# One activation table set in the front of a hybrid RWKV-7 and FoX trunk layer, with group norm, inverse and output split rearranged

## The chip, the cores and the metric

The kernel runs on one NeuronCore of one Trainium2 chip. The core has a matmul engine (PE; its weight loads are shown apart as PEld), a vector engine (DVE), an activation engine (ACT), GpSimd (POOL) and a queue that issues DMAs (SP). Each engine takes its own instructions in the order in which they were placed, and waits on semaphores for the others. The metric is device microseconds of one execution, the median of several runs; lower is better.

## The reference

One layer of a streaming encoder: 512 tokens after 16 meta tokens (T = 528), model width 1024, all in float32. After an RMS norm, one input projection of 5384 columns feeds two branches and the gates.

```
u = rmsnorm(h);  proj = u @ w_in
w_log = -softplus(-(w0 + tanh(wd) @ w_lora_up)) - 0.5        # decay of RWKV-7
decay = exp(-exp(w_log));  a = sigmoid(a0 + ad @ a_lora_up);  g = sigmoid(gd) @ g_lora_up
kk = k*k_k / max(||k*k_k||, 1e-12);  k = k*(1 + (a-1)*k_a)
S_t = S_{t-1}(diag(w_t) + a_t^T b_t) + v_t^T k_t;  y_t = S_t r_t     # 8 heads of 64
y_rw = (groupnorm(y)*lnx_g + lnx_b + bonus) * g
y_fx = softmax(q k^T/8 + F_q - F_k, causal) @ v              # FoX, 8 heads of 64, q and k normed
merged = sigmoid(gA)*(y_rw @ w_out_rw) + sigmoid(gB)*(y_fx @ w_out_fx)
h = h + merged @ w_o;  h = h + relu(rmsnorm(h) @ w_up)^2 @ w_down   # 4096 wide
```

## The kernel before

**Precision.** A float32 product of the large matmuls is made from three passes: each operand is split into a rounded part (hi, a cast on ACT) and the rest (lo, a subtraction on DVE or POOL), and PE adds hi*hi, hi*lo and lo*hi. `load_h` (L255) loads a weight tile of 128x512, casts it on ACT (L261) and subtracts on DVE (L262); `convert` (L466) does so for the input projection with the subtraction on POOL (L471, L472); `split` (L284) does it for activations (L285, L286).

**The front** (up to about 500 us) is a set of Python generators, "streams", that emit instructions in turns. `Turns.run` asks each stream, in order of rank, when the operands of its next piece will be ready; a planner (`Clock`) estimates that from a cost for each instruction emitted so far, without table loads. The first stream whose time plus `ROOM[rank]` has come goes on; a rank in `AHEAD` also has its DVE, ACT, POOL and DMA work placed earlier by that many steps of priority. PE's order is the order of emission and is never changed; the other engines are ordered by priority. The streams and their ranks:

- rank 0, `chain(g, prs)` (L939): the recurrence of a group of two head pairs over nine chunks of 64 tokens. A step fetches what was saved of the chunk from DRAM (`rec`, L948), multiplies with the state (L972), with the chunk's inverse (L978, `recs[pr_][hs, 448:]`), makes the new state (L990, L992) and the outputs (L998, L1001, L1002). For the second group it starts only when the first group's norm is finished (`yield normalised[0][1]`).
- rank 1, `recurrent` (L1040): for pairs 0 to 3 `decay` (two sigmoids, by `AF.Tanh` at L744, and the running product of decays), `keys`, `rows`, `scores`, and after every second pair `group`: `inverse(g, ...)` (L856), which inverts nine triangular matrices for each head into the tile `Tt` and saves them to `rec_d` in DRAM (`save(..., 448, 512, Tt)`), then adds the chain.
- rank 2, `attention`; rank 3, `fox_features` (norms of q and k, L570 to L575); rank 4, `group_norm` (L1008), called after chunks 4 and 8 of each chain; rank 8, `projections` (L476), 40 blocks of the input projection (matmuls at L500), of which the 16 gate blocks come last and fill what the others leave.
- rank 6, `fox_merged`: after the last projection it takes over the buffers `uhi` and `ulo` of the projection's input, splits `y_fx` into them (`part`), and multiplies with the FoX half of the output weights (L1103), gates the result (tanh at L1096, L1104) and writes it to DRAM (L1105). Rank 5, `rw_split`, splits `y_rw` into the same buffers as the group norms of group 1 finish.

**ACT's tables.** A function of ACT needs its table set loaded; a load is an instruction of its own on ACT (ACT_TABLE_LOAD). Before each Ln the kernel places a load of the set that has exp and ln (`pinned`, L280), after the instruction named, and the compiler adds further loads where an instruction's function isn't in the set that its order leaves there.

**After the front** the pools of the front are closed; then come the RWKV half of the output weights (L1151, with the gates' tiles `gl`), `w_o` (L1181, L1198) and the MLP (L1232, L1265).

Of the kernel before, what the change touches and what calls it, by code (L numbers as in the profile page):

```python
# [185 lines left out]
class Turns:  # L186
# [4 lines left out]
    AHEAD = {0: 100, 1: 40, 2: 20, 3: 20}  # L191
    ROOM = {0: 0.0, 1: 1.0, 2: 1.0, 3: 1.5, 4: 2.5, 5: 0.0, 6: 0.0, 8: 0.5}
# [32 lines left out]
def kernel(ctx, tc, ht, x, win, par, cst, gain, lora, wout, wo, wup, wdn, out, dbg=None):  # L225
# [24 lines left out]
    prh = cp.tile([128, 4, 4], F32, name="prh")  # L250
# [43 lines left out]
    rec_d = [dr.tile([NCH, 128, 512], F32, name=f"rec{i}") for i in range(4)]  # L294
# [5 lines left out]
    with ExitStack() as st:  # L300
# [103 lines left out]
        V.tensor_scalar(prh[:, 0, :], pr[:, C_W0:C_W0 + 4], 0.5, None, ALU.mult)  # L404
        V.tensor_scalar(prh[:, 1, :], pr[:, C_A0:C_A0 + 4], 0.5, None, ALU.mult)
        V.tensor_scalar(prh[:, 2, :], pr[:, C_KA:C_KA + 4], 0.5, None, ALU.mult)
        V.tensor_scalar(prh[:, 3, :], pr[:, C_KA:C_KA + 4], -0.5, 1.0, ALU.mult, ALU.add)
# [19 lines left out]
        act(gf, gf, AF.Tanh, scale=0.5)  # L427
# [108 lines left out]
        def fox_features():  # L536
            for p in range(4):
# [5 lines left out]
                def ask_normed(blk, parts, name):  # L543
                    d = {}

                    def begin():
# [4 lines left out]
                        def finish():  # L551
                            G.tensor_tensor(f, f, rs[:, c0:], ALU.mult)
                            d["s"] = act(sq[:, c0:], f, AF.Square)
# [8 lines left out]
                def normed(d, parts, gcol):  # L562
# [3 lines left out]
                    pin = None  # L566
                    for a0, a1 in parts:
                        pq = psm("pssq")[:, :a1 - a0]
                        for hs in hss:
                            mm(pq[hs], ones_blk[hs, hs], sq[hs, a0:a1], start=True, stop=True)  # L570
                        pin = pin or pinned(d["s"])
                        after(act(sq[:, a0:a1], pq, AF.Ln, bias=eps, scale=1.0 / 64), pin)
# [134 lines left out]
        normalised = [[Event(), Event()] for g in range(2)]  # L707

        class Pair:
# [20 lines left out]
            def decay(self):  # L730
# [6 lines left out]
                for a0, a1 in ((0, HT), (HT, T)):  # L737
# [5 lines left out]
                    for i in range(2):  # L743
                        act(dst[i][:, a0:a1], pos[i], AF.Tanh, bias=prh[:, i, p:p + 1], scale=0.5)  # L744
                V.tensor_scalar(dst[0], dst[0], 0.5, 0.5, ALU.mult, ALU.add)
# [8 lines left out]
            def keys(self):  # L754
# [4 lines left out]
                s_ = act(sq[:, :T], okr, AF.Square, scale=self.col(C_KK))  # L759
# [6 lines left out]
                pin = pinned(s_)  # L766
                after(act(sq[:, :T], sq[:, :T], AF.Ln), pin)
                act(sq[:, :T], sq[:, :T], AF.Exp, scale=-0.5)
                V.tensor_scalar(kp[:, PADT:], thr, prh[:, 2, p:p + 1], prh[:, 3, p:p + 1], ALU.mult, ALU.add)
# [5 lines left out]
                V.scalar_tensor_tensor(BK[:, :, 2, :], kkn, 0.5, pinv, ALU.mult, ALU.mult)  # L775
                V.scalar_tensor_tensor(BK[:, :, 0, :], tha3, 1.0, BK[:, :, 2, :], ALU.add, ALU.mult)
# [79 lines left out]
        def inverse(g, prs):  # L856
# [11 lines left out]
            if g > 0:  # L868
                for r0, r1 in low:
                    G.memset(Tt[r0, :, :, 32:64], 0.0)  # L870
# [23 lines left out]
            Tt2 = Tt.rearrange("p a b c -> p (a b) c")  # L894
            Dn, W2 = (AX_[:, i, :].rearrange("p (a b) -> p a b", b=64) for i in (1, 0))
# [33 lines left out]
            for pr_ in range(2):  # L929
# [7 lines left out]
                prs[pr_].save(slice(0, 128), 448, 512, Tt[:, pr_])  # L937

        def chain(g, prs):  # L939
# [4 lines left out]
            def fetch_rec(c):  # L944
                recs = []
                for q in prs:
                    t = rp.tile([128, 512], F32, name="rec", bufs=4)
# [16 lines left out]
            for c in range(NCH):  # L964
# [11 lines left out]
                for pr_ in range(2):  # L976
                    for hs in hss:
                        mm(ch[hs, 1, pr_, :], recs[pr_][hs, 448:], Rs[hs, pr_], start=True, stop=True)  # L978
# [24 lines left out]
                if c in (4, 8):  # L1003
                    turns.add(4, group_norm(g, y[:, :, c - 4:c, :], c - 4, prs, lws))
                if nxt is not None:
                    uv, recs = nxt, nxt_recs

        def group_norm(g, y, c0, prs, lws):  # L1008
# [9 lines left out]
            after(act(st2, st2, AF.Ln, bias=epsg, scale=1.0 / 64), pinned(s_))  # L1018
# [21 lines left out]
        def recurrent():  # L1040
# [4 lines left out]
            def group(g, ev):  # L1045
                yield from inverse(g, pairs[2 * g:2 * g + 2])
                turns.add(0, chain(g, pairs[2 * g:2 * g + 2]))
                ev.done = True
            pairs[0].ask_keys()
            pairs[0].ask_values()  # L1050
            for p, q in enumerate(pairs):
# [19 lines left out]
                if j == 1:  # L1071
                    turned_in = Event()
                    turns.add(1, group(g, turned_in))
            yield normalised[1][1]

        merge = []
        fox_split = Event()

        def part(k, c0, c1):
            split(merge[0][:, k, c0:c1], merge[1][:, k, c0:c1], (y_rw, y_fx)[k // 4][:, k % 4, c0:c1])  # L1080

        def fox_merged():

            yield projected
            for name in ("uhi", "ulo"):
                merge.append(up.tile([128, KB, S], F32R, name="y" + name, tag=name))
            turns.add(5, rw_split())
            for p in range(4):
                yield fox_done[p]
                part(4 + p, 0, S)  # L1090
            w = load_h(wout[0][:, 512:], V, "w", (WR, WH, WH))
            for m in range(KB):
                cur, w = w, load_h(wout[m + 1][:, 512:], V, "w", (WR, WH, WH)) if m < KB - 1 else None
                g = fp.tile([128, S], F32, name="gf", tag="qa", bufs=2)
                nc.sync.dma_start(g, gates_d[8 + m])
                act(g, g, AF.Tanh, bias=bgh[:, 8 + m:9 + m], scale=0.5)  # L1096
                po = None
                for k in range(4):
                    yield lambda f=po is None: max(ck.ready(*cur, merge[0][:, 4 + k, :], merge[1][:, 4 + k, :]), ck.ring("pj", 1, 2) if f else 0.0)
                    if po is None:  # L1100
                        po = ppj("pj")
                    for n, (a, b) in enumerate(passes([x[:, 128 * k:128 * k + 128] for x in cur], merge)):
                        mm(po, a, b[:, 4 + k, :], start=k == 0 and n == 0, stop=k == 3 and n == 2)  # L1103
# [3 lines left out]
        def rw_split():  # L1107
            for k in range(2):
                part(k, 0, S)
            for i in range(2):  # L1110
# [237 lines left out]
```

## Time and profile before

| | us |
|---|---|
| median of 3 runs (lowest to highest) | 932.55 (931.81 to 932.99) |
| the profiled execution, its own time | 933.79 |
| its span, first to last instruction | 932.0 |
| PE busy / DVE busy / ACT busy / POOL busy | 876.4 / 451.2 / 461.6 / 200.1 |
| mean granted clock of PE | 0.97 |

In the profile a group row reads: line, engine, operation, out<-in, shapes, count, then busy time, mean ns of one, idle time of the engine before them and what ended it. A wait row reads: who waited <- for whom: total us, times, longest. A row of stretches reads: stretch, its length, busy time of PE, PEld, DVE, ACT and POOL (with instructions), the granted PE clock, the DMA share and GB/s. A row of the timeline reads: start, duration, engine, line, operation. PE's busy time counts matmuls that overlap, so that a busy PE isn't a PE at its peak.

### The profile page before, as it was taken

The numbers are of one execution on the slowest core, as the hardware profiler recorded it, in microseconds if no ns is written. First come the engines' busy times: TensorE is split into PE (matmuls) and PEld (weight loads), VectorE is DVE, ScalarE is ACT, GpSimd is POOL, SyncE is SP. The second block draws the span as 40 slices with busy tenths as digits, with TensorE's granted clock in tenths as the row PEclk, the third lists the DMA queues.
The fourth block names the chain that finished last, engine by engine and source line by source line (L and its number), as shares of the span: only waits on it lengthen the run. The fifth ranks groups of instructions, "written<-read, shape, count | busy, mean of one in ns | idle before, by whom it ended". The sixth has DMA issues, their size and how long they took to land.

```text
span 932.0 us, 15719 instructions
## 1 busy us (share of the span) xinstructions
PE 876.4 (94%) x5968; PEld 717.4 (77%) x5968; DVE 451.2 (48%) x850; ACT 461.6 (50%) x941; POOL 200.1 (21%) x202
## 2 busy tenths in 40 slices
PE   7899898799898999999888899999999999999998
PEld 6888686587677877866566688988888888888886
DVE  6573546823546583345365665445423244543321
ACT  7755853765577536568554463344322234442220
POOL 1374453362515537231100210000000000000000
PEclk9999989899999999999989899999999999999999
DMA  6344246123574545234377760123223232322331
GB/s 218 93 124 129 63 115 169 39 95 103 162 213 137 119 133 179 66 112 135 115 236 260 249 215 12 46 95 98 99 94 102 91 102 94 99 101 92 119 97 46
DMA packets 94044, 113.26 MB, mean 122 GB/s; under 512 B 26888, under 2 KB 47624, under 8 KB 93968
## 3 DMA queue, kind: packets, MB, share of 16 engines
q1 hardware_dynamic: 93968, 112.25, 38.9%
q8 instruction: 47, 0.77, 0.3%
q14 instruction: 29, 0.24, 0.1%
HBM read 90.97 MB, written 20.07 MB: 119 GB/s over the span
## 4 chain that ended last, share of the span: by engine, by line
PE 68%; DVE 9%; ACT 9%; DMA 4%; issue 3%; POOL 3%; SPq 2%; POOLq 0%; ACTq 0%; DVEq 0%
PE po L1232 19%; PE pd L1265 19%; PE pj L500 11%; PE po L1181 3%; PE po L1198 2%; PE pj L1103 2%; DMA wraw<-in_win 2%; PE pw L907 1%; POOL wlo L472 1%; DVE tmp L889 1%; PE po L1151 1%; DVE AX L890 1%; ACT whi L471 1%; PE psc L637 1%; PE pj L390 1%
## 5 line engine op out<-in xcount | busy, mean ns | idle before, releaser
L261 ACT CAST whi<-wraw 128x512 fp32r<-128x512 f32 x152 | 93.8, 622 | 196.8 <-PE pd L1265 105.5
L262 DVE TENSOR_TENSOR wlo<-wraw,whi 128x512 fp32r<-128x512 f32 x152 | 104.3, 691 | 173.8 <-ACT whi L261 171.0
L500 PE MATMUL pj<-uhi,whi 128*128 128x264 f32 (+1 forms) x480 | 168.5, 351 | 3.2 <-ACT tm L328 3.2
L500 PE MATMUL pj<-uhi,wlo 128*128 128x264 f32 (+1 forms) x480 | 157.0, 327 | 0.0
L500 PE MATMUL pj<-ulo,whi 128*128 128x264 f32 (+1 forms) x480 | 157.0, 327 | 0.0
L472 POOL TENSOR_TENSOR wlo<-wraw,whi 128x512 fp32r<-128x512 f32 x80 | 107.7, 1358 | 127.1 <-ACT whi L471 109.4
L500 PEld LDWEIGHTS pj<-uhi,whi 128*128 128x128 f32 x480 | 93.1, 194 | 27.2 <-issue 13.2
L1265 PE MATMUL pd<-whi,fhi 128*128 128x512 f32 x256 | 99.6, 389 | 0.0
L1265 PE MATMUL pd<-wlo,fhi 128*128 128x512 f32 x256 | 99.6, 389 | 0.0
L1265 PE MATMUL pd<-whi,flo 128*128 128x512 f32 x256 | 99.6, 389 | 0.0
L500 PEld LDWEIGHTS pj<-uhi,wlo 128*128 128x128 f32 x480 | 93.0, 194 | 7.2
L500 PEld LDWEIGHTS pj<-ulo,whi 128*128 128x128 f32 x480 | 93.3, 194 | 5.0
L1232 PE MATMUL po<-zhi,whi 128*128 128x512 f32 (+1 forms) x248 | 94.8, 382 | 0.0
L1232 PE MATMUL po<-zlo,whi 128*128 128x512 f32 (+1 forms) x248 | 94.8, 382 | 0.0
L1232 PE MATMUL po<-zhi,wlo 128*128 128x512 f32 (+1 forms) x248 | 94.8, 382 | 0.0
L471 ACT CAST whi<-wraw 128x512 fp32r<-128x512 f32 x80 | 48.2, 620 | 33.2 <-DMA wraw<-in_win 18.2
L1265 PEld LDWEIGHTS pd<-wlo,fhi 128*128 128x128 f32 x256 | 48.0, 188 | 10.1
L1265 PEld LDWEIGHTS pd<-whi,flo 128*128 128x128 f32 x256 | 48.0, 188 | 9.9
L1265 PEld LDWEIGHTS pd<-whi,fhi 128*128 128x128 f32 x256 | 48.0, 188 | 9.9
L1232 PEld LDWEIGHTS po<-zhi,wlo 128*128 128x128 f32 x248 | 46.6, 188 | 9.1
L1232 PEld LDWEIGHTS po<-zlo,whi 128*128 128x128 f32 x248 | 46.6, 188 | 9.0
L1232 PEld LDWEIGHTS po<-zhi,whi 128*128 128x128 f32 x248 | 46.6, 188 | 8.9
(313 smaller groups left out, 1472.0 us busy)
## 6 DMA issues: line engine op xcount, KB each, us to landing
wraw<-in_win SPq DMA_DIRECT2D x84, 256.0 KB, 3.2
wraw<-in_wup SPq DMA_DIRECT2D x64, 256.0 KB, 2.6
wraw<-in_wdn SPq DMA_DIRECT2D x64, 256.0 KB, 2.5
rec<-rec SPq DMA_DIRECT2D x36, 256.0 KB, 3.0
gd<-gt SPq DMA_DIRECT2D x16, 256.0 KB, 2.1
wraw<-in_wout SPq DMA_DIRECT2D x16, 256.0 KB, 3.1
gl<-gd SPq DMA_DIRECT2D x16, 256.0 KB, 3.1
wraw<-in_wo SPq DMA_DIRECT2D x16, 256.0 KB, 4.8
```

The lines of the kernel that those rows point to most:

```text
L261: A.copy(hi, raw)
L262: low.tensor_tensor(lo, raw, hi.bitcast(F32), ALU.subtract)
L390: mm(dst, a, b[:, k, cols], start=n == 0, stop=n == 23)
L471: A.copy(hi, raw)
L472: G.tensor_tensor(lo, raw, hi.bitcast(F32), ALU.subtract)
L500: mm(po, a, b[:, k, a0:a1], start=n == 0, stop=n == 23)
L637: mm(sc, q[hs, 128 * i:128 * i + 128], k[hs, a:b], start=True, stop=True)
L1103: mm(po, a, b[:, 4 + k, :], start=k == 0 and n == 0, stop=k == 3 and n == 2)
L1181: mm(pd[i], a[:, k, 128 * i:128 * i + 128], b, start=k == 0 and n == 0, stop=k == 7 and n == 2)
L1198: mm(po, a[:, k, 128 * i:128 * i + 128], b[:, k, :], start=n == 0, stop=n == 23)
L1232: mm(po[:, t0:t1], a, b[:, k, t0:t1], start=n == 0, stop=n == 23)
L1265: mm(pd[i], a[:, b_, 128 * i:128 * i + 128], b, start=b_ == 0 and n == 0, stop=b_ == 15 and n == 2)
```

## The change

1. The two sigmoids of `decay` are made as 1/(1+exp(-x)): exp on ACT, then min with 1e37 and plus 1 on DVE, Ln on ACT, Exp of the negative on ACT, for each of the two 128x528 tiles. Before: tanh, and for one of them one multiply-add. The constants in `prh` and the formulas for `kp` and `BK` follow.
2. The loads of the exp-and-ln set placed ahead of the Ln in `fox_features`, `keys` and the first group's `group_norm` go; one is placed after the tanh at the start. The second group's `group_norm` keeps its own.
3. `group_norm` gets rank 1, next to the chain; recurrent, attention and features move down to ranks 2, 3 and 4 with about the AHEAD and ROOM they had.
4. The inverse stays in `Tt` in SBUF: no save, `rec` is 448 columns wide instead of 512, and the chain's matmul (L978) reads `Tt`. So that the second group doesn't write `Tt` too early, its inverse waits for the event `chained` (the first chain is emitted to its end), and the clearing of `Tt` moves behind that wait.
5. `y_fx` is split, as each pair's attention is done, into eight tiles of the recurrence's pool (`okk`, `ov`, `orr`, `lc`, `sg`, `P`, `tha`, `sq`), after the event `inverted` (the second inverse is emitted). `merge` holds only `y_rw`. In `fox_merged` the weights and the gate tile of the next block are asked for one block ahead, and the gate tiles use the buffers of `qa` and `ka` in turn.

```diff
-    AHEAD = {0: 100, 1: 40, 2: 20, 3: 20}
-    ROOM = {0: 0.0, 1: 1.0, 2: 1.0, 3: 1.5, 4: 2.5, 5: 0.0, 6: 0.0, 8: 0.5}
+    AHEAD = {0: 100, 1: 40, 2: 40, 3: 20, 4: 20}
+    ROOM = {0: 0.0, 1: 1.0, 2: 1.0, 3: 1.0, 4: 1.5, 5: 0.0, 6: 0.0, 8: 0.5}
...
-        act(gf, gf, AF.Tanh, scale=0.5)
+        pinned(act(gf, gf, AF.Tanh, scale=0.5))
...
-                        pin = pin or pinned(d["s"])
-                        after(act(sq[:, a0:a1], pq, AF.Ln, bias=eps, scale=1.0 / 64), pin)
+                        act(sq[:, a0:a1], pq, AF.Ln, bias=eps, scale=1.0 / 64)
...
                     for i in range(2):
-                        act(dst[i][:, a0:a1], pos[i], AF.Tanh, bias=prh[:, i, p:p + 1], scale=0.5)
-                V.tensor_scalar(dst[0], dst[0], 0.5, 0.5, ALU.mult, ALU.add)
+                        act(dst[i][:, a0:a1], pos[i], AF.Exp, bias=prh[:, i, p:p + 1], scale=-1.0)
+
+                for d in dst:
+                    V.tensor_scalar(d, d, 1e37, 1.0, ALU.min, ALU.add)
+                    act(d, d, AF.Ln)
+                    act(d, d, AF.Exp, scale=-1.0)
...
-                pin = pinned(s_)
-                after(act(sq[:, :T], sq[:, :T], AF.Ln), pin)
+                act(sq[:, :T], sq[:, :T], AF.Ln)
                 act(sq[:, :T], sq[:, :T], AF.Exp, scale=-0.5)
-                V.tensor_scalar(kp[:, PADT:], thr, prh[:, 2, p:p + 1], prh[:, 3, p:p + 1], ALU.mult, ALU.add)
+                V.tensor_scalar(kp[:, PADT:], thr, self.col(C_KA), prh[:, 2, p:p + 1], ALU.mult, ALU.add)
...
-                V.scalar_tensor_tensor(BK[:, :, 2, :], kkn, 0.5, pinv, ALU.mult, ALU.mult)
-                V.scalar_tensor_tensor(BK[:, :, 0, :], tha3, 1.0, BK[:, :, 2, :], ALU.add, ALU.mult)
+                V.tensor_tensor(BK[:, :, 2, :], kkn, pinv, ALU.mult)
+                V.tensor_tensor(BK[:, :, 0, :], tha3, BK[:, :, 2, :], ALU.mult)
...
             Tt2 = Tt.rearrange("p a b c -> p (a b) c")
+            if g > 0:
+                yield chained
+                for r0, r1 in low:
+                    G.memset(Tt[r0, :, :, 32:64], 0.0)
...
-                prs[pr_].save(slice(0, 128), 448, 512, Tt[:, pr_])
...
-                    t = rp.tile([128, 512], F32, name="rec", bufs=4)
+                    t = rp.tile([128, 448], F32, name="rec", bufs=4)
...
-                        mm(ch[hs, 1, pr_, :], recs[pr_][hs, 448:], Rs[hs, pr_], start=True, stop=True)
+                        mm(ch[hs, 1, pr_, :], Tt[hs, pr_, c, :], Rs[hs, pr_], start=True, stop=True)
...
                 if c in (4, 8):
-                    turns.add(4, group_norm(g, y[:, :, c - 4:c, :], c - 4, prs, lws))
+                    turns.add(1, group_norm(g, y[:, :, c - 4:c, :], c - 4, prs, lws))
...
+            chained.done = True
...
-            after(act(st2, st2, AF.Ln, bias=epsg, scale=1.0 / 64), pinned(s_))
+            ln = act(st2, st2, AF.Ln, bias=epsg, scale=1.0 / 64)
+            if g > 0:
+                after(ln, pinned(s_))
...
+        def fox_split():
+
+            yield inverted
+            for p in range(4):
+                yield fox_done[p]
+                pieces = [rp.tile([128, S], F32R, name="yf", tag=t) for t in (("okk", "ov"), ("orr", "lc"), ("sg", "P"), ("tha", "sq"))[p]]
+                split(*pieces, y_fx[:, p, :])
+                halves.append(pieces)
+
+        def rw_split():
             yield projected
             for name in ("uhi", "ulo"):
-                merge.append(up.tile([128, KB, S], F32R, name="y" + name, tag=name))
-            turns.add(5, rw_split())
-            for p in range(4):
-                yield fox_done[p]
-                part(4 + p, 0, S)
-            w = load_h(wout[0][:, 512:], V, "w", (WR, WH, WH))
+                merge.append(up.tile([128, 4, S], F32R, name="y" + name, tag=name))
+            yield normalised[0][1]
...
+        def fox_merged():
+
+            yield projected
+
+            def load(m):
+                if m == KB:
+                    return None
+                g = fp.tile([128, S], F32, name="gf", tag=("qa", "ka")[m % 2], bufs=2)
+                nc.sync.dma_start(g, gates_d[8 + m])
+                return load_h(wout[m][:, 512:], V, "w", (WR, WH, WH)), g
+            yield fox_done[3]
+            nxt = load(0)
             for m in range(KB):
-                cur, w = w, load_h(wout[m + 1][:, 512:], V, "w", (WR, WH, WH)) if m < KB - 1 else None
-                g = fp.tile([128, S], F32, name="gf", tag="qa", bufs=2)
-                nc.sync.dma_start(g, gates_d[8 + m])
+                (w, g), nxt = nxt, load(m + 1)
                 act(g, g, AF.Tanh, bias=bgh[:, 8 + m:9 + m], scale=0.5)
...
+        turns.add(5, fox_split())
+        turns.add(5, rw_split())
         turns.add(6, fox_merged())
-        turns.add(1, recurrent())
-        turns.add(2, attention())
-        turns.add(3, fox_features())
+        turns.add(2, recurrent())
+        turns.add(3, attention())
+        turns.add(4, fox_features())
```

54 lines of the change are left out of this document (26 added, 28 removed).

## The prediction

> **What bounds the kernel now.** I read the page first (span and busy times), then the stretches, then who waited on PE, then the clock around the long waits, then ACT's groups there and the chain that ended last.
>
> ```profile
> span 932.0 us, 15719 instructions
> 0.00:462.20 462.20, 424.73 (x3916) 343.17 (x3916) 245.07 (x538) 288.61 (x639) 187.76 (x193) 0.96 0.43 126
> 462.20:500.90 38.70, 27.89 (x125) 22.29 (x125) 23.96 (x42) 23.23 (x44) 1.26 (x1) 0.91 0.65 214
> 500.90:552.90 52.00, 48.52 (x193) 39.23 (x194) 29.95 (x42) 26.67 (x44) 11.06 (x8) 0.90 0.76 246
> 552.90:932.00 379.10, 375.27 (x1736) 312.73 (x1735) 152.18 (x230) 123.12 (x216) 0.00 (x0) 1.00 0.27 89
> ```
>
> These are four stages: the front to the last input projection, the FoX half of the output weights (L1103), the gates with the first half of `w_o`, and the rest. The last is 379.1 us of PE at full clock; the change touches nothing there. What can move is in the first 501 us. PE is busy 425 of 462 us in the front, the other engines two fifths to two thirds: the front is limited by PE, which takes its work in a fixed order, with holes where an operand is late. The projections fill it to its end. So a step counts only where a hole in PE closes; an engine that merely gets faster under PE's cover is worth nothing. The holes:
>
> ```profile
> PE pj L1103 <- ACT whi L261: 6.3, 1, 6.3
> PE pch L990 <- ACT uv L980: 5.7, 6, 2.0
> PE psc L637 <- DVE pT L667: 5.5, 1, 5.5
> PE psc L637 <- DVE ka L575: 5.4, 1, 5.4
> PE po L1151 <- DVE gf L1104: 3.0, 1, 3.0
> PE pup L742 <- ACT sg L744: 1.9, 1, 1.9
> PE pj L1103 <- DVE gf L1104: 1.0, 1, 1.0
> ```
>
> A hole costs more than its length, since the granted clock falls to half behind it (the figure behind POOL's count is the clock that was granted):
>
> ```profile
> 112.60:118.00 5.40, 0.01 (x1) 0.01 (x1) 5.05 (x5) 5.34 (x9) 3.86 (x5) 0.72 0.50 109
> 118.00:121.80 3.80, 3.80 (x12) 2.77 (x13) 3.35 (x8) 2.81 (x7) 3.28 (x4) 0.50 0.02 6
> 281.30:285.60 4.30, 4.26 (x38) 3.65 (x39) 1.46 (x4) 3.14 (x9) 1.26 (x1) 0.61 0.61 193
> 468.40:473.40 5.00, 4.46 (x10) 3.06 (x11) 4.11 (x7) 2.53 (x5) 0.00 (x0) 0.50 0.43 147
> 473.40:478.40 5.00, 5.00 (x27) 4.17 (x26) 3.36 (x6) 2.12 (x5) 0.00 (x0) 1.00 0.84 282
> ```
>
> After the hole that ends at 468.4, PE starts 10 matmuls in 5 us, in the next 5 us 27.
>
> **The split of y_fx and the weights asked for ahead.** This stands at the seam between the first two stages. The chain that ended last runs there so:
>
> ```profile
> 463.06 1.28 ACT L280
> 465.27 2.59 ACT yuhi L285 x5
> 467.86 1.57 ACT whi L261 x3
> ...
> 495.92 3.28 DMA gf<-gd
> ...
> 500.06 0.70 DVE gf L1104
> 500.90 9.93 PE po L1151 x36
> ```
>
> A table load, five casts of y and three casts of weights stand in ACT's order between the last projection and the first L1103. The change moves the casts of `y_fx` and their subtractions ahead, to where each pair's attention ends, and the weights are no longer behind them. Then L1103 can follow the last projection: 6.3 us of hole, 0.5 us in which PE wasn't busy behind it (5.00 less 4.46), and half of the 4.46 us at half clock, 2.2. I leave 0.5 for what stays. That is 8.5 us. The moved ACT and DVE work (four casts and subtractions, the same count) lies in the front under PE's cover, so I cost it at nothing; without that cover it is the 2.59 us of casts that the chain shows.
>
> In L1103 itself the gate tile came late from DRAM (3.28 us, just ahead of its tanh and L1104), because two buffers are shared by load, tanh, product and write-back. With four buffers and the load a block earlier the 1.0 us wait goes, and of the 3.0 us ahead of L1151 only PE's end to the end of one L1104 (0.70 plus a hop) must remain: I take 2.0. Sum of the seam: 8.5 + 1.0 + 2.0 = 11.5 us. SP's queue gets the same sixteen DMAs earlier; its waits are not PE's. The group norm at rank 1 belongs to this term: its last pieces now stand between the matmuls of L1103, and L1151 needs them; with the chain earlier they are done before. The seam's bounds are 0, if a new wait stands there, and 14.7: everything above with nothing left over (6.3 + 0.5 + 2.2 + 1.0 + 3.0 = 13.0, and 1.7 of clock loss as behind the hole at 281).
>
> **One table set.** Loads on ACT between 94 and 117 us, around the third hole:
>
> ```profile
> L572 ACT ACT_TABLE_LOAD x2 | 2.6, 1283 | 0.0
> L280 ACT ACT_TABLE_LOAD x1 | 1.3, 1283 | 0.0
> L744 ACT ACT_TABLE_LOAD x1 | 1.3, 1283 | 0.0
> L767 ACT ACT_TABLE_LOAD x1 | 1.3, 1283 | 2.7 <-DVE sq L765 2.7
> L768 ACT ACT_TABLE_LOAD x1 | 1.3, 1283 | 0.0
> L750 ACT ACT_TABLE_LOAD x1 | 1.3, 1283 | 0.0
> L574 ACT ACT_TABLE_LOAD x1 | 1.3, 1283 | 0.0
> L767 ACT ACTIVATE sq<-sq x4: 638/642/647, 49.1 to 293.8; 128x528 f32<-128x528 f32 x4
> L745 DVE TENSOR_SCALAR sg<-sg x4: 422/1174/1519, 44.4 to 284.7; 128x528 f32<-128x528 f32 x4
> ```
>
> Eight loads, 8 x 1.283 = 10.3 us, all go. Added to each pair are Ln and Exp for two tiles of 528, 4 x 0.642 = 2.6 us on ACT, and one more DVE instruction like L745, 0.4 to 1.5 us. ACT gains 7.7 us here. The hole and its half clock are 5.4 + 3.80/2 = 7.3 us, and the gain lies between nothing (another operand is late instead) and 7.3. I take 4: DVE is itself busy 5.05 of the 5.40 us of the hole, and becomes the late one. In the last pair's `decay` L742 waits 1.9 us for L744, of which one load is 1.28; with the clock behind it (0.39 x 4.30 = 1.7) at most 3.6, I take 2. The other loads of the front lie under PE's cover: nothing, with the 5.7 us of L990's six waits as upper end, and as lower end the longer sigmoid (the rival below).
>
> By the Trainium skill (ScalarE: Activation LUTs, "What ACT_TABLE_LOAD costs") a switch costs 2.66 us, a load of 1283 ns and a drain of about 1380 ns. The load agrees with the rows; the drain doesn't show, as ACT is busy 5.34 of 5.40 us across two loads. By the page's price ACT would gain 18.7 us here, the hole's 7.3 would go whole, and the sum would be 3.3 us better.
>
> **Group norm, inverse, ranks.**
>
> ```profile
> 295.81 0.45 PE L978 MATMUL pch<-Rs,rec 64*64 64x64 f32 x8
> 348.29 2.07 DVE L901 COPY Tt<-TT 32x576 f32<-32x576 f32 x2
> 386.16 1.33 PE L934 MATMUL pw<-Tt,W 32*32 32x32 f32 x72
> 411.65 0.45 PE L972 MATMUL pch<-uv,rec 128*64 128x64 f32 x8
> ```
>
> The new wait `chained` asks that the first chain's last use of the inverse (295.8) precede the second group's first write to `Tt` (348.3): 52 us of room, so nothing is held; behind it stand only that group's inverse and the clearing on POOL. The second inverse ends at 387, its chain starts at 411.7, because it waits for the first group's norm, at rank 4 until now; the saved inverse's way through DRAM is in there too, four saves with SP waiting behind them. The change brings this chain some 20 us forward. PE has projections to do there and to 462 anyway, so I cost that at nothing in time; if the gates' projections ran out, this same lead would be the cover. The 36 loads of `rec` shrink by an eighth, on queues that PE's waits don't name. The new AHEAD and ROOM keep the old figures for the old streams, so I give them no price.
>
> **Sum.** 11.5 + 4 + 2 = 17.5 us. The profiled execution took 933.79 us around its span of 932.0; that gives 916.3. The median of the runs shown is 1.24 us lower, so 915.
>
> **Rivals**, in terms of the median, 932.55.
>
> *The seam alone.* PE's order is planned anew, and the holes of the front reappear at other operands: 932.55 - 11.5 = 921. For it speaks the DVE row of the hole.
>
> *The front closes up.* Beside the sum also L990's 5.7, the rest of the two holes (3.3 and 1.6) go, and the 5.5 us of L637 behind DVE: 16.1 more at most, half of it gives 907. For it: eight loads go within 23 us here alone; against: L667 stands behind the inverse on DVE, which stays.
>
> *Slower: the sigmoid in three passes.* If the recurrence, not PE, were the bound, each pair's path would grow by 4 x 0.642 + 1.17 = 3.7 us, four pairs by 15, with the loads beside the path: the seam's 11.5 is lost and 3.5 more, 936. It decides from 11.5/4 = 2.9 us a pair. Against it: 25 us between the second inverse and its chain. The Trainium skill (ScalarE: Activation LUTs, "Step-by-step: what each stage is for") says that every function costs the same for each element; the rows agree (L744's tanh and the logarithm follow the width), so that three passes are three times the work.
>
> ```profile
> L1096 ACT ACT_TABLE_LOAD x3: 1283/1283/1283, 403.6 to 481.0; - x3
> L680 ACT COPY y_fx<-py x16: 243/265/271, 182.7 to 453.6; 128x128 f32<-128x128 f32 x16
> ```
>
> *The tables come back.* The first tanh of a gate was placed at 403.6, amid the front. Without the pins each later Ln and Exp would need a load, and a hole like the 7.3 us returns: 915 + 7.3 = 922.
>
> *y_fx too late.* Attention now ranks behind the group norm. Its last block ends at 453.6, 8.6 us ahead of the last projection. If it slipped by 18 us, PE would stand some 10 us with a clock loss of 2 at the seam: 915 + 12 = 927; by 24 us and the change makes no difference.
>
> **How the numbers follow.** The sum 0.44; the seam alone 0.20; the front closes up 0.14; slower 0.11; tables 0.05; y_fx late 0.06. The likeliest is 915, its own range 909 to 921. The range 903 to 928 leaves out the slower case, the end of the closed-up one and a bad y_fx, together under 0.2. A change of 0.2%, 1.9 us, is about what a measurement of this kernel can tell from none. Faster: 0.44 + 0.20 + 0.14 + 0.05 + half of y_fx late = 0.86; the same 0.03; slower 0.11.
>
> **What would show it.** In the changed profile L1103 starts within 1 us of the last L500, at full clock, and L1151 within 1.5 us of the last L1103; no load of a table stands between 60 and 390 us; L637's wait for `ka` is under 2 us; the second chain's first L972 stands within 5 us of the last L934 of its inverse; 552.9 to the end keeps its 379 us. The prediction is wrong if the wait ahead of L1103 remains under another name (a split placed late on ACT or DVE), or if PE's waits before the seam sum to more than before.

## Result and the profile after

The changed kernel takes 936.41 us (median of 20 runs, 932.72 to 938.62) against 934.23 us for the kernel before on the same chip (20 runs, 931.80 to 938.97): a ratio of 1.0011 [0.9995, 1.0026], no difference that this can tell. Forecast were 915 us and a gain. The profiled execution took 932.72 us, 3.7 below its median, with a span of 930.9. The ratios here and below leave out runs of a disturbed, slower state, of which one, of the kernel before in another order, took 1686.79 us.

The stages after, cut at the same events as in the prediction (stretch, length, busy time of PE, PEld, DVE, ACT and POOL, granted clock, DMA share, GB/s):

```profile
0.00:468.10 468.10, 424.76 (x3944) 344.72 (x3944) 258.26 (x555) 272.39 (x648) 190.82 (x193) 0.97 0.42 121
468.10:499.10 31.00, 25.42 (x98) 19.97 (x97) 17.84 (x29) 14.50 (x26) 1.27 (x1) 0.89 0.73 237
499.10:551.30 52.20, 46.38 (x192) 36.56 (x192) 29.89 (x41) 25.35 (x41) 10.64 (x8) 0.97 0.76 248
551.30:930.90 379.60, 375.60 (x1737) 313.01 (x1736) 152.59 (x230) 123.59 (x218) 0.00 (x0) 1.00 0.28 89
```

The second stage became 7.7 us shorter (38.70 to 31.00), the last two stayed (52.00 and 379.10 before), and the front became 5.9 us longer (462.20 to 468.10) at the same PE busy time, 424.76 against 424.73. ACT lost 16.2 us of work there (288.61 to 272.39), and PE got nothing for it. PE's waits after:

```profile
PE pj L499 <- ACT tm L328: 13.3, 3, 6.2
...
PE pch L992 <- ACT uv L982: 4.5, 7, 1.0
PE pj L499 <- ACT qa L555: 4.2, 2, 2.6
PE po L1202 <- ACT whi L261: 3.9, 1, 3.9
PE pj L1130 <- ACT whi L261: 3.5, 1, 3.5
PE pssq L568 <- DVE pT L664: 3.5, 1, 3.5
...
PE pssq L568 <- DVE nm L643: 2.7, 1, 2.7
...
PE po L1172 <- DVE gf L1131: 1.1, 1, 1.1
```

The two holes of the front that the prediction wanted closed are closed: L637's wait for `ka` (5.4) and the pup wait for `sg` (1.9) are no longer there, nor is L637's wait for `pT` (5.5), which its sum left in place. New ones stand in their place, one of 3.5 us for `pT` at another line among them. The largest is new altogether: projections (L499) that wait for the copy of a block before them out of PSUM, the memory that PE's results land in (`tm`, L328), 13.3 us in three waits, where the kernel before had four short ones:

```profile
PE pj L500 <- ACT tm L328: 3.2, 4, 1.1
```

ACT around the longest of them (start, duration, engine, line, operation, shapes, and in brackets the idle time before and what ended it):

```profile
171.83 0.65 ACT L747 ACTIVATE sg<-sg 128x528 f32<-128x528 f32 x1 [4.36 <-DVE sg L746]
...
177.81 0.68 ACT L752 ACTIVATE P<-lc 128x576 f32<-128x576 f32 x1 [2.48 <-DVE lc L750]
178.40 0.36 ACT L328 COPY tm<-pj 128x264 f32<-128x264 f32 x1
```

The copy takes 0.36 us and stands in ACT's order behind steps of `decay` that wait for DVE, 4.36 us for the new DVE step and 2.48 us for the scan.

### The profile page after: what moved, and what is told of

It reads as the page before. It is cut to its first block, busy times and chain, and to the rows that moved or that the text cites. A ratio compares the mean times of both kernels' runs of the same rounds, so it can differ in the third digit from the quotient of the medians.

```text
span 930.9 us, 15708 instructions
## 1 busy us (share of the span) xinstructions
PE 872.2 (94%) x5968; PEld 714.3 (77%) x5968; DVE 458.6 (49%) x853; ACT 435.8 (47%) x932; POOL 202.7 (22%) x202
## 4 chain that ended last, share of the span: by engine, by line
PE 58%; DVE 5%; DMA 4%; ACT 2%; SPq 1%; issue 1%; POOL 1%; DVEq 0%; ACTq 0%; POOLq 0%
PE po L1253 19%; PE pd L1286 19%; PE pj L499 7%; PE po L1202 2%; PE po L1219 2%; PE pj L1130 2%; DMA gl<-gd 1%; DVE tmp L888 1%; PE pw L910 1%; DMA gf<-gd 1%; DMA nF<-fF_d 1%; DVE AX L889 1%; PE py L676 0%; DMA wraw<-in_wo 0%; PE psc L634 0%
## 5 line engine op out<-in xcount | busy, mean ns | idle before, releaser
L262 DVE TENSOR_TENSOR wlo<-wraw,whi 128x512 fp32r<-128x512 f32 x152 | 107.3, 709 | 170.6 <-ACT whi L261 169.0
L499 PE MATMUL pj<-uhi,whi 128*128 128x264 f32 (+1 forms) x480 | 168.4, 351 | 17.5 <-ACT tm L328 13.3
L499 PE MATMUL pj<-uhi,wlo 128*128 128x264 f32 (+1 forms) x480 | 157.3, 328 | 0.4 <-POOL wlo L471 0.4
L499 PE MATMUL pj<-ulo,whi 128*128 128x264 f32 (+1 forms) x480 | 157.1, 327 | 0.0
L471 POOL TENSOR_TENSOR wlo<-wraw,whi 128x512 fp32r<-128x512 f32 x80 | 110.0, 1385 | 149.5 <-ACT whi L470 139.2
L499 PEld LDWEIGHTS pj<-uhi,whi 128*128 128x128 f32 x480 | 93.5, 195 | 38.7 <-ACT tm L328 13.9
L499 PEld LDWEIGHTS pj<-uhi,wlo 128*128 128x128 f32 x480 | 93.6, 195 | 7.8 <-POOL wlo L471 0.8
L499 PEld LDWEIGHTS pj<-ulo,whi 128*128 128x128 f32 x480 | 93.9, 196 | 4.5
L1286 PEld LDWEIGHTS pd<-whi,flo 128*128 128x128 f32 x256 | 48.0, 188 | 10.1
```

Source lines behind the costliest of these rows:

```text
L262: low.tensor_tensor(lo, raw, hi.bitcast(F32), ALU.subtract)
L471: G.tensor_tensor(lo, raw, hi.bitcast(F32), ALU.subtract)
L499: mm(po, a, b[:, k, a0:a1], start=n == 0, stop=n == 23)
L1286: mm(pd[i], a[:, b_, 128 * i:128 * i + 128], b, start=b_ == 0 and n == 0, stop=b_ == 15 and n == 2)
```

## Experiments

The theories: **T1**, the longer sigmoid costs the front what the loads give back, and the norm moves work from the seam to the front; **T2**, the forecast; **T3**, PE's order, which the planner makes anew for every edit, moves the time by several us by itself. All ratios are to the kernel before, with a 95% interval.

**The parts one at a time.** Each is applied to the kernel before, without the others.

Only part 5 of the change, `y_fx` split early and weights ahead:

```diff
-        merge = []
+        merge, halves = [], []
+        turns.add(5, fox_split())
+        turns.add(5, rw_split())
```

> The kernel before with part 5 alone (y_fx split into the recurrence's buffers, weights and gate tile asked for a block ahead). Theory 1, the seam gains and the front pays: the front keeps its length (last projection near 462 us), the hole ahead of the first FoX matmul shrinks from 6.3 us to about 3.5 (the six casts of y_rw now stand where the casts of y_fx stood), and the kernel is 3 to 6 us faster, ratio 0.994 to 0.997. Theory 2, the seam's gain isn't there at all and something else holds it: ratio 0.999 to 1.002. Theory 3, any new order moves the front by several us either way: the last projection is off 462 by more than 3 us.

Measured: 928.63 us, 0.9954 [0.9935, 0.9972], 4.3 us of the 11.5 forecast. Only parts 1 and 2, one table set:

```diff
-                        act(dst[i][:, a0:a1], pos[i], AF.Tanh, bias=prh[:, i, p:p + 1], scale=0.5)
+                        act(dst[i][:, a0:a1], pos[i], AF.Exp, bias=prh[:, i, p:p + 1], scale=-1.0)
...
-                        after(act(sq[:, a0:a1], pq, AF.Ln, bias=eps, scale=1.0 / 64), pin)
+                        act(sq[:, a0:a1], pq, AF.Ln, bias=eps, scale=1.0 / 64)
```

> The kernel before with parts 1 and 2 alone (one table set, three-pass sigmoid). Theory 1, the longer sigmoid (DVE, ACT, ACT ahead of the scan) costs the front what the loads give: last projection at 462 to 466 us, ratio 1.000 to 1.005, and a PE hole of about 6 us near 173 us behind ACT's copy of a projection. Theory 2, fewer loads shorten the front as forecast: last projection at 455 to 457 us, ratio 0.993 to 0.995.

Measured: 943.13 us, 1.0119 [1.0096, 1.0141]; a loss of 11 us in place of a gain of 6. Only part 4, the inverse in SBUF:

```diff
-                        mm(ch[hs, 1, pr_, :], recs[pr_][hs, 448:], Rs[hs, pr_], start=True, stop=True)
+                        mm(ch[hs, 1, pr_, :], Tt[hs, pr_, c, :], Rs[hs, pr_], start=True, stop=True)
...
-                prs[pr_].save(slice(0, 128), 448, 512, Tt[:, pr_])
```

> The kernel before with part 4 alone (inverse stays in SBUF, narrower records). Under PE's cover: ratio 0.998 to 1.002 by every theory but the third; if the order alone moves the front, off by 3 us or more in either direction.

Measured: 924.42 us, 0.9899 [0.9876, 0.9922], a gain of 9.4 us from what the forecast gave no price. The first chain starts 12 us earlier; the group of L972 in the kernel before and the same line in this one (duration min/median/max in ns, first and last start in us):

```profile
L972 PE MATMUL pch<-uv,rec x144: 219/222/367, 232.6 to 456.7; 128*64 128x64 f32 x144
```

```profile
L974 PE MATMUL pch<-uv,rec x144: 219/222/271, 220.5 to 469.2; 128*64 128x64 f32 x144
```

SP's queue in the kernel before held the saves of the inverse back for 33.6 us in all, and these two rows are gone in this one:

```profile
SPq L809 <- ACT Tt L936: 16.9, 4, 7.7
SPq L809 <- DVE Tt L919: 16.7, 2, 9.9
```

Only part 3, the norm next to the chain:

```diff
-                    turns.add(4, group_norm(g, y[:, :, c - 4:c, :], c - 4, prs, lws))
+                    turns.add(1, group_norm(g, y[:, :, c - 4:c, :], c - 4, prs, lws))
...
-        turns.add(1, recurrent())
+        turns.add(2, recurrent())
```

> The kernel before with part 3 alone (group norm at rank 1, the others one rank down). The second chain starts some 15 us earlier. Theory 1: the four pieces of the second group's norm (0.8 us of PE each, 3.2 us) move from the seam into the front, so the last projection is 3 us later and the seam 3 us shorter, and with the wait of 3.0 us ahead of L1151 smaller the ratio is 0.997 to 1.000. Theory 2, the norm next to the chain delays the chain and attention: last projection over 468 us, ratio over 1.003.

Measured: 941.41 us, 1.0103 [1.0078, 1.0128]. The four ratios multiply to 1.0073 where the whole has 1.0011, and none is near the forecast for its part.

**Parts together.** Parts 4 and 5, then all but part 3, both as in the diffs above:

```diff
+            chained.done = True
...
+        turns.add(5, fox_split())
```

> The kernel before with parts 4 and 5, without the table set and the norm's rank. If the parts add up: 0.9954 x 0.9899 = 0.985, some 919 to 920 us. If the order alone makes the time (each new order a new draw of holes), the sum doesn't hold: 0.990 to 1.000.

Measured: 923.56 us, 0.9888 [0.9864, 0.9912]. The product of the parts would be 0.9853. L637 still waits 5.4 us for `ka` and 6.7 us for `pT` here: the kernel that is 10 us faster keeps the holes that the prediction priced.

```diff
-                V.tensor_scalar(dst[0], dst[0], 0.5, 0.5, ALU.mult, ALU.add)
+                    act(d, d, AF.Exp, scale=-1.0)
...
+            chained.done = True
+        turns.add(5, fox_split())
```

> The changed kernel without the norm's rank (parts 1, 2, 4, 5). If the parts add up: 0.9954 x 0.9899 x 1.0119 = 0.997, 931 us. Theory 1 (the longer sigmoid lies on the recurrence's path and is a cost of its own): slower than the kernel with parts 4 and 5 alone by about 1.2%. Theory 3 (order alone): anything from 0.988 to 1.005.

Measured: 940.00 us, 1.0068 [1.0044, 1.0092]. The norm's new place loses 1% on the kernel before, and taken out of the changed kernel it leaves that one slower too. A part that costs 1% in one neighbourhood and gains 0.6% in another has no price of its own: T1's "moves 3.2 us" falls.

**The sigmoid with the planner free.** Parts 1 and 2 alone, so with the loads gone, but one pass in place of the sigmoid, so that the decay and the rate are no sigmoids then (shown against part 1):

```diff
-                        act(dst[i][:, a0:a1], pos[i], AF.Exp, bias=prh[:, i, p:p + 1], scale=-1.0)
-                for d in dst:
-                    V.tensor_scalar(d, d, 1e37, 1.0, ALU.min, ALU.add)
-                    act(d, d, AF.Ln)
-                    act(d, d, AF.Exp, scale=-1.0)
+                        act(dst[i][:, a0:a1], pos[i], AF.Identity, bias=prh[:, i, p:p + 1], scale=-0.01)
+                V.tensor_scalar(dst[0], dst[0], 0.01, 0.5, ALU.mult, ALU.add)
```

> Parts 1 and 2 alone, but with one ACT pass of the same width (Identity) in place of exp, and one DVE instruction in place of the two with their Ln and Exp: the decay and the in-context rate are not sigmoids here. So the loads are gone and nothing is paid for it. Theory 1, the three-pass sigmoid is what costs: the loss of 1.2% goes and the loads' gain shows, ratio 0.990 to 0.997. Theory 3, the loads under PE's cover are worth nothing and the new order is what costs: ratio 1.000 to 1.010, with a hole of 5 us or more behind the second inverse.

Measured: 928.79 us, 0.9934 [0.9912, 0.9956]. By itself this speaks for T1, and more than it seems: though free, the planner gave this kernel the order of the kernel before (of the 5968 matmuls in each trace all but two stand in the same place), so that the loads are taken out here at a fixed order. Next, the DVE step folded into the logarithm, first in the changed kernel, then without part 3:

```diff
-                    V.tensor_scalar(d, d, 1e37, 1.0, ALU.min, ALU.add)
-                    act(d, d, AF.Ln)
+                    act(d, d, AF.Ln, bias=1.0)
```

> The changed kernel whole, with the DVE step of the sigmoid (min and add) folded into the bias of the logarithm, so that Exp, Ln and Exp follow each other on ACT without a crossing to DVE; the guard of 1e37 is left out. T1 (the length of the sigmoid's chain costs the time): the 6.2 us hole ahead of the projections (L499 <- ACT tm) falls to 4 or less and the ratio to the kernel before to 0.990 to 0.997. T1b (not the DVE crossing but ACT's extra passes, which stand ahead of the rescaled copies in ACT's order, cost it): no more than 0.3% better than the changed kernel, 0.998 to 1.002. T2 (the forecast): 1.00 to 1.002, the sigmoid has no part. T3 (order alone): anywhere between 0.99 and 1.01.

> One table set, the inverse in SBUF and the FoX split (without the group norm's new place; 1.0068 with the DVE step), with the DVE step of the sigmoid folded into the logarithm's bias; the guard of 1e37 is left out. T1 (chain length): 0.990 to 0.998. T1b (ACT's passes): 1.003 to 1.007. T3: 0.99 to 1.01, with no relation to the step taken out.

Measured: 926.23 us, 0.9916 [0.9892, 0.9939], and 944.95 us, 1.0112 [1.0091, 1.0134]. The same edit gains 0.95% in the one and loses 0.4% in the other (1.0068 before it). And in the first, where T1 has its number, the hole that the step was to close is still there:

```profile
PE pj L499 <- ACT tm L328: 14.2, 3, 6.4
```

So these gains and losses need not be those of the edit; the runs with the order held (below) decide. A first test of T3 had changed the planner's tolerance in the kernel before:

```diff
-    SLACK = 0.15
+    SLACK = 0.25
```

> The kernel before with the planner's SLACK at 0.25 us instead of 0.15: the same instructions, another order of PE's streams. It measures how far an order alone moves the time. Theory 3: off by 4 us or more (0.4%) in either direction, with holes at other operands. By theories 1 and 2 (each part has a price of its own): within 0.3% of 1.

Measured: 933.99 us, 0.9994 [0.9971, 1.0018]. I took that as evidence against T3; it shows only that one other order is as good.

**The casts at the seam.** The split of `y_rw` one rank behind the FoX products, in the changed kernel and in parts 4 and 5 alone:

```diff
-        turns.add(5, rw_split())
+        turns.add(7, rw_split())
```

> The changed kernel whole, with the split of the recurrent y moved one rank behind that of the FoX y, so that its six casts on ACT cannot stand ahead of the cast of the output weight. T1: the hole of 3.5 us ahead of the first output projection matmul goes under 1 us, but half of it comes back where the recurrent half is wanted; 0.997 to 1.001. T2: the whole 3.5 us and the 3.9 us wait of the last sum go, 0.992 to 0.995. T3: no statement.

> The kernel before with the inverse in SBUF and the FoX split alone (0.9888 as measured) and the split of the recurrent y one rank behind. T1: the wait of 5.3 us for the weight's cast falls to under 2, 0.984 to 0.988. T2: the same. T3: 0.98 to 0.995.

Measured: 937.82 us, 1.0029 [1.0012, 1.0047], and 923.38 us, 0.9880 [0.9858, 0.9903]. The first missed its aim: all six casts still stand ahead of the weight's.

```profile
473.34 2.36 ACT L285 CAST yuhi<-y_rw 128x512 fp32r<-128x512 f32 x6
475.60 1.14 ACT L261 CAST whi<-wraw 128x512 fp32r<-128x512 f32 x2
```

The second is the fastest here, though not apart from the 0.9888 of parts 4 and 5; its wait for the weight's cast fell from 5.3 to 4.4 us, not to under 2.

**The order held fixed.** The planner's choices (651 turns in the kernel before) were written down and given to other kernels, whose streams have the same number of turns. PE's instructions then stand in exactly that order; the other engines still follow their priorities.

```diff
-            at = next((i for i, t in enumerate(times) if t + self.ROOM[self.streams[i][0]] <= ck.pe + ck.SLACK), None)
-            if at is None:
-                at = min(range(len(times)), key=lambda i: times[i])
+            at = next(i for i, s in enumerate(self.streams) if s[1] == ORDER[self.turn])
+            self.turn += 1
```

First both directions between the kernel before and parts 1 and 2 alone:

> One table set alone, with the planner's list of turns taken from the kernel before, so that TensorE's 3,859 rows stand in exactly the order of before (the free planner gave this part another order and 1.0119). T1 (the longer sigmoid itself costs what the loads give back and more): 1.005 to 1.012. T2 (the forecast, minus 6 us): 0.993 to 0.996. T3 (the new order did it): 0.993 to 1.001.

> The kernel before, with nothing changed in what it computes or how, and with the list of turns that the planner gave to one table set alone. T1: the order has no part, 0.998 to 1.003. T2: the same. T3: 1.005 to 1.015.

Measured: one table set in the order of before, 936.48 us, 1.0025 [1.0003, 1.0048]; the kernel before in the order of one table set, 944.93 us, 1.0101 [1.0070, 1.0131]. Nothing in the second one's instructions is changed, and it loses nearly all that one table set had lost. The two kernels with that order, one table set (first row) and the kernel before (second), even have the same longest wait in common, which the kernel before doesn't have in its own order:

```profile
PE ppt L660 <- ACT fsq L569: 7.7, 1, 7.7
```

```profile
PE ppt L663 <- ACT fsq L572: 7.7, 1, 7.7
```

ACT in the second of them shows what the order does:

```profile
365.06 3.49 ACT L900 COPY AX<-AX 32x576 f32<-32x576 f32 x3 [0.67 <-POOL AX L896]
368.57 0.58 ACT L521 COPY gt<-pj 128x512 f32<-128x512 f32 x1
369.18 1.17 ACT L900 COPY AX<-AX 32x576 f32<-32x576 f32 x1
370.38 0.85 ACT L572 ACTIVATE fsq<-pssq,small 128x264 f32<-128x264 f32 x2
```

The second inverse comes later in this order (its products at 394 us instead of 372), and its four copies, 4.66 us, fall just ahead of the logarithm (L572) for which PE waits. The clock is at half from 368 to 375 behind that hole.

Then two edits of the changed kernel in its own order: tables and sigmoids as before, and the DVE step alone.

> The changed kernel with the sigmoids, the scale factors and the pins of the kernel before (35 table loads), in the order of turns of the changed kernel (1.0011). T1: faster than the changed kernel, 0.990 to 0.996. T2: slower by the forecast's 6 us, 1.006 to 1.010. T3: about the changed kernel's, 0.998 to 1.006.

> The changed kernel with the DVE step of the sigmoid folded into the logarithm's bias (the guard of 1e37 is left out), in the order of turns of the changed kernel; with the planner free the same edit gave 0.9916. T1: 0.992 to 0.998. T2: 1.000 to 1.002. T3: 0.998 to 1.002, what the free planner gained was the order.

Measured: 934.33 us, 0.9997 [0.9978, 1.0017], and 934.72 us, 1.0010 [0.9987, 1.0033]. With the order held, the old sigmoids with their 24 table loads more (34 instead of 10) give the same time as the new ones without, within 0.25%, and the DVE step is worth nothing that shows: the 0.9916 of the free planner was its order. The holes only change owner. With the tables undone these stand, among others, where the changed kernel has its 13.3 us for `tm`:

```profile
PE py L676 <- DVE nm L646: 5.0, 1, 5.0
...
PE psc L637 <- DVE ka L575: 3.7, 1, 3.7
PE pj L500 <- ACT tm L328: 3.5, 5, 1.5
```

Last, the one pass in the order of before (same edit as above), and the whole changed kernel in the order of parts 4 and 5:

> One table set with a single Identity pass in place of the sigmoid (decay and rate are no sigmoids then), under the order of turns of the kernel before; with the planner free it gave 0.9934, and the whole sigmoid under the same order 1.0025. T1 (sigmoid): 0.985 to 0.994, the loads are worth what the forecast said and the sigmoid takes it. T2 (the forecast): 0.993 to 0.996. T3 (order): 0.996 to 1.001, the loads are worth little and most of 0.9934 was order.

> The changed kernel, all its instructions, with the list of turns that the planner gave to the inverse in SBUF and the FoX split alone (0.9888). T1: 0.997 to 1.003, the changed kernel's own loss goes with its instructions. T2: 0.982 to 0.986. T3: 0.986 to 0.992, the order carries the gain and the loss, and the four parts together cost nothing by themselves.

Measured: 928.13 us, 0.9915 [0.9882, 0.9948], and 929.20 us, 0.9928 [0.9905, 0.9951].

The first separates loads and sigmoid at a fixed order. Without the loads and with a sigmoid of one pass the kernel gains 0.85%, 7.9 us; the three passes then cost 1.0025/0.9915 = 1.1%, 10.3 us. The earlier run of one pass is the same program: its trace has the same instructions in the same order on PE, ACT, DVE and POOL (5968, 917, 849 and 202). So replaying the list costs nothing that shows, and there are two measures, 6.2 us (0.9934) and 7.9 for the loads, some 8.5 and 10.3 for the passes. T1 is right in size after all in this order, but both effects together are 2.3 us. Where the sigmoid's cost can arise is seen in the stretch 82 to 100 us, in the kernel before, with three passes, and with one (columns as above):

```profile
82.00:100.00 18.00, 16.88 (x132) 14.89 (x132) 5.01 (x10) 11.59 (x23) 3.94 (x3) 0.91 0.47 140
```

```profile
82.00:100.00 18.00, 12.78 (x82) 11.82 (x80) 5.21 (x10) 5.23 (x13) 2.96 (x2) 0.72 0.47 133
```

```profile
82.00:100.00 18.00, 15.79 (x109) 13.89 (x109) 5.28 (x10) 8.62 (x20) 2.99 (x3) 0.81 0.49 141
```

PE gets through 132, 82 and 109 matmuls. DVE shows why: the last `Mt` of the pair, and the step L323 behind which the projections' copies stand on ACT; three passes first, then one:

```profile
79.19 0.56 DVE L837 TENSOR_TENSOR Mt<-psr,cs 128x384 f32<-128x384 f32 x1 [2.54 <-DMA rec<-Mt]
...
86.24 0.86 DVE L875 COPY Ain<-M 32x288 f32<-32x288 f32 x2 [1.22 <-DMA M<-Mt]
87.12 0.71 DVE L323 TENSOR_TENSOR tm<-tm,rs 128x528 f32<-128x528 f32 x1
```

```profile
73.67 0.56 DVE L834 TENSOR_TENSOR Mt<-psr,cs 128x384 f32<-128x384 f32 x1 [1.45 <-PE pbt L848]
...
82.53 0.91 DVE L872 COPY Ain<-M 32x288 f32<-32x288 f32 x2 [1.21 <-DMA M<-Mt]
83.47 0.71 DVE L323 TENSOR_TENSOR tm<-tm,rs 128x528 f32<-128x528 f32 x1
```

The matrices of the pair are 5.5 us later; the copies of the inverse (`Ain`) wait on DVE for their DMA, and L323, which has nothing to do with them, waits behind them and is 3.7 us later. PE then stands for 5.2 us instead of 2.2, and the clock is at half for 10 us instead of 7:

```profile
89.93 0.59 PE L499 MATMUL pj<-uhi,whi 128*128 128x264 f32 x1 [5.22 <-ACT tm L328]
```

```profile
86.28 0.39 PE L499 MATMUL pj<-uhi,whi 128*128 128x264 f32 x1 [2.21 <-ACT tm L328]
```

The next `decay` starts 4.9 us later (101.9 against 97.0), and by the last one this difference has grown only to 5.7 (283.0 against 277.3). These are single executions, and one program can differ from itself by as much. The earlier run of the same one-pass program went through the stretch at full clock:

```profile
82.00:100.00 18.00, 16.68 (x141) 14.10 (x140) 5.99 (x12) 10.44 (x24) 6.87 (x6) 1.00 0.50 146
```

Its next `decay` starts at 91.8 us, 5.2 before that of the other execution, its last at 275.8, and its span is only 0.7 us shorter. So how much arises in this stretch isn't settled. What holds against both executions is that the three passes are behind at the second `decay` (4.9 and 10.1 us) and about as far or less behind at the last (5.7 and 7.2): the cost arises in the first pair, not four times.

The second run is T3's number: all instructions of the changed kernel, in another order, take 7.8 us less (0.9928 against 1.0011), and it is then faster than the kernel before. Against the 0.9888 of parts 4 and 5 in the same order, parts 1 to 3 cost 0.4%.

How the losses of PE stand, worked out from the traces up to 345 us before the last matmul: gaps of over 0.6 us between matmuls, and half of the matmul time in stretches where the granted clock was half.

| | gaps, us | half clock, us | matmuls otherwise, us |
|---|---|---|---|
| before | 42.7 | 23.4 | 508.0 |
| before, order of one table set | 46.0 | 28.5 | 507.9 |
| one table set | 50.0 | 27.9 | 507.9 |
| one table set, order of before | 48.3 | 20.3 | 508.1 |
| one pass, order of before | 41.6 | 19.5 | 507.9 |
| the same one-pass program, earlier run | 42.7 | 18.1 | 507.2 |
| changed kernel | 45.2 | 15.6 | 511.6 |
| changed kernel, order of parts 4 and 5 | 40.5 | 19.7 | 511.4 |

The work is the same to within 4 us, and everything else is gaps and the clock behind them. Each row is of one profiled execution, that of the changed kernel 3.7 us below its median and the one under it 4.2 us above, and the two rows of the one-pass program differ by up to 1.4 us in a column. So the table places the losses, and the ratios carry the verdicts.

**Left open.** Parts 3, 4 and 5 change the number of turns or the ranks, so their ratios (1.0103, 0.9899, 0.9954) hold their own effect and that of a new order, and weren't taken apart. Nor is it settled why one order is 1% better than another, beyond the single holes shown.

## Why the prediction was wrong

**One table set, 4 + 2 us.** The mechanism was right where it was looked at: no load stands between 41 and 424 us, the waits for `ka` and `sg` went. The step that failed is the price of what was added, "The other loads of the front lie under PE's cover: nothing", with the sigmoid as lower end only. At the order of the kernel before the loads give 6.2 and 7.9 us in two runs, about the 6 forecast or a little more, and the sigmoid takes some 8.5 to 10.3. The prediction counted 2.6 us of ACT and 0.4 to 1.5 us of DVE per pair as engine time, set them against 10.3 us of loads, and wrote "ACT gains 7.7 us here". But engine time isn't what PE waits for: in the rows above the three passes stand in a chain of dependent steps, at whose end DVE waits for a DMA with a step of the projections behind it.

**The rival with the sigmoid** named the time, 936, but by another mechanism: a loss of 3.7 us in each of four pairs. The runs show no loss added after the second pair's start, and in the changed kernel's own order no net loss against the old sigmoids with their loads (0.9997 against 1.0011).

**The planner's order** was no term of the sum. "PE's order is planned anew" stood in a rival as a way to lose 6 us of gain; the order alone is worth 9.4 us between two orders of the kernel before, and 7.8 between two of the changed one. The time came out 18.5 us from the forecast (17.5 gained against 1.0 lost). The order accounts for 7.8 of these where that of parts 4 and 5 is the measure, in which the change gains 6.7 us; the other 11 or so are missing in that order too, and lie in the terms. Neither order is the right one to measure by, so this division holds for these two alone.

**The seam, 11.5 us.** Alone, with the new order that it brings, it gave 4.3. The hole is 3.5 us in the changed kernel, not under 1, with a granted clock of 0.54 behind it:

```profile
468.24 0.59 ACT L520 COPY gt<-pj 128x512 f32<-128x512 f32 x1 [4.18 <-PE pj L499]
468.72 2.36 ACT L285 CAST yuhi<-y_rw 128x512 fp32r<-128x512 f32 x6
470.99 1.14 ACT L261 CAST whi<-wraw 128x512 fp32r<-128x512 f32 x2
```

```profile
472.00:479.00 7.00, 6.07 (x15) 4.46 (x14) 4.26 (x8) 3.21 (x6) 0.00 (x0) 0.54 0.79 257
```

The prediction took the casts of `y_fx` away and put nothing in their place. The casts of `y_rw`, which still need the buffers of the projections, took it: six at once, since the norm is now done by then. What is late next had not been asked. The wait ahead of L1172 fell to 1.1 us, as forecast, but a new one of 3.9 us came at L1202, where a weight's cast is late again.

**Norm, inverse, ranks, nothing.** The second chain starts as its inverse ends, at 400 us instead of 412, as said; the first starts at 220 instead of 233 in the changed kernel too, which wasn't said, though the rows of SP's waits for `Tt` were in the trace. Alone, with the new order each brings, the inverse gave 9.4 us and the norm took 9.6. "PE has projections to do there and to 462 anyway" is no price: counted as in the table, the matmuls outside the half clock stayed within 2.4 us (508.0 before, 510.4 and 509.0 with the inverse and the norm alone), while gaps and half clock together went from 66.1 to 54.4 and to 77.3.

**The signs named** for a wrong prediction both came: the wait for the weight's cast stayed, and PE's gaps before the last projection sum to 33.9 us where they were 28.9 (those over 0.6 us, up to 468 and up to 462 us). Of the six signs named for a right one five came all the same, all but L1103 within 1 us of the last projection: they watched the holes that were priced, and not what would stand in their place.

The Trainium skill (ScalarE: Activation LUTs, "What ACT_TABLE_LOAD costs") counts a drain of some 1380 ns for each load. It doesn't show in these traces: behind 32 of the 35 loads of the kernel before ACT goes on after 0.01 us. An estimate by it for the 24 loads fewer of the one-pass kernel is 64 us of ACT. By the 1.283 us of the rows it is 31 us; what they were worth in time, at a fixed order, is 6.2 to 7.9 us.

## What to carry to other kernels

Where an edit lets a planner order the work anew, hold the order fixed first (write its choices down and replay them, in both directions), or see in the traces whether the order changed at all: else a ratio of 1% says nothing of the edit. Before a stretch of one profile is read as a cause, look at a second execution of the same program. Price a longer chain by who stands behind its last step in an in-order engine, not by the engine time it adds; and price a removed instruction by what it delayed, not by its length. When something is taken away ahead of a wait, ask which instruction that was waiting for the same thing moves into its place.

## What was unexpected of the hardware

Time removed from ACT didn't become time: 16.2 us less of it in the front, with PE's busy time the same to 0.03 us. The granted clock made short holes expensive: behind the 4.6 us hole at 84 us in the changed kernel it stayed at half for 10 us, in which PE was busy 8.38 us, a loss of 4.2 us, nearly as much as the hole; behind that of 2.2 us in the one-pass kernel for 7 us.

```profile
87.00:97.00 10.00, 8.38 (x48) 7.92 (x49) 2.80 (x5) 4.03 (x11) 2.97 (x2) 0.50 0.51 163
```
